# The last layer's 32 gate, query and key projections in a Strassen stage of their own, handed on through DRAM

## The chip, the cores and the metric

One Trainium2 chip, one core of it. The metric is device time in microseconds for one execution, compared between the kernel before and the kernel after. No collective is involved; what follows is one instruction stream on each of TensorE (PE), VectorE (DVE), ScalarE (ACT) and GpSimd (POOL), and one queue of DMAs issued by SyncE (SP).

## The reference

Two blocks run on 1024 tokens of width 1024 (fp32). The first block has an attention layer, an MLP, an LRU layer and a second MLP; the second block has one layer, the last of the kernel and the one the change is about:

```
x = rms_norm(x, final_norm)                      # end of the first block
h = x @ w_in      # q 512, k 512, v 1024, gate_a 1024, alpha 16, pool_in 1024, gate_b 1024, merge 2048
log_alpha = log_sigmoid(alpha_low @ w_alpha_up + b_alpha) / 16
o   = _gla_chunked(q / sqrt(128), k, v, log_alpha)       # 4 heads, dk 128, dv 256, chunks of 64
y_a = headwise_norm(o) * gla_norm_g * silu(gate_a)
y_b = _multiscale_pool(pool_in, w_pool_grp, pool_scale) * silu(gate_b)
g_a, g_b = split(sigmoid(merge + b_merge))
y   = (g_a * (y_a @ w_proj_a) + g_b * (y_b @ w_proj_b)) @ w_out
out = layernorm(2**0.25 * x + y)
```

An MLP of the first block is `square(relu(h @ w_up)) @ w_down`. The final norm's factor per token is applied after the projections, since `(x * rs) @ w = rs * (x @ w)`.

## The kernel before

Activations lie transposed: eight tiles `x[k]` of 128 features by 1024 tokens. Every fp32 operand is split into two fp32r parts, `wh, wl` for weights and `xgh, xgl` (called `X`) for the normed activations; a product is three matmuls (`mm3`, lines 154 to 156: high by high, high by low, low by high). An **m-tile** is 128 output features of a projection for all 1024 tokens: `gemm` (line 160) makes 2 halves of 512 columns x 8 k x 3 = 48 matmuls of 128x512 for it. Its weights come by one DMA of 512 KB (`wdma`), one ACT copy (line 122) and one DVE subtraction (line 124).

The stages follow each other in program order, each with its own split of the eight PSUM banks. What matters here:

- `mlp_up` (line 645): the up projection by Strassen's algorithm in Winograd's form. 32 m-tiles, in pairs. The first two pairs are made directly (`up(m)`, 4 x 48 matmuls) while DVE and ACT build the sums of quarters of `X` (`sums`: T1, T2, T3, T4). T4 is written over the upper halves (tokens 512 to 1023) of X[0] to X[3] (line 726). Then 14 `unit`s, each a pair of m-tiles, do 7 products of 4 k x 3 matmuls of 128x512 where a direct pair would do 8. `load(u)` forms four half sums of the weights on DVE, and `finish` squares and spills what the down projection needs, with four adds on POOL.
- `gla_mix` (line 1046): the last layer up to `y_b @ w_proj_b`. Its first lines split and square x (`norm`). Then generators are woven: **fills**, which give PE dense work, and **chains**, which are long dependent sequences of small work.
  - Fills (`fill_steps`, line 1216), 40 steps: merge gates 0 to 7; then for each head h two tiles of gate_a, two of pool_in, two of gate_b (with the 256x256 map of the pool group), two more merge gates. Merge gates and gate_a go to DRAM and come back later.
  - `decays` (line 1081): alpha projection, log-sigmoid, a scan per head, spill of G; then `z_tokens` transposes x (all eight tiles still held) into the residual.
  - `qkv(h)` (line 1129): two m-tiles (q, k) and v in eight blocks of 24 matmuls of 128x256. It comes before chain h.
  - `chain(h, q, k, v)` (line 1244), 18 steps: six levels, each POOL differences of G (lines 1268, 1269), ACT exp, DVE q and k products (1271, 1272), PE scores (1253) into one tile `sc` by DVE copies (1260); then eight steps of the running state (PE 1322 to 1327, DVE 1332), a norm, and the scaling by gate_a (1356).
  - The order: 3 fills and the first step of the decays, decays with 5 fills, then for h = 0, 1, 2 `qkv(h)` and chain h with 9 fills, then `qkv(3)`, the first 9 steps of chain 3 with the last 5 fills, then the rest of chain 3, then `merge_b`.
- `merge_b` (line 1378) reads y_b back from DRAM, splits it (lines 256, 257) and makes 8 m-tiles; `merge_out` follows.

The Tile framework turns this into queues: it orders each engine's instructions by program order and by a simulated time, so a later instruction can stand ahead of an earlier one that is not ready there. On the chip each engine then keeps its order. Buffers of 128x1024: 31 of tag A (`a`), 8 of tag B (`b`), and 2 `ws`, 5 `wh`, 5 `wl` for weights. An instruction that needs a buffer waits for the last reader of its former content. X takes 16 of the 31.

Of the kernel before, what the change touches and what calls it, by code (L numbers as in the profile page):

```python
# [8 lines left out]
F32 = mybir.dt.float32  # L9
# [36 lines left out]
class Core:  # L46
# [151 lines left out]
    def stats(self, accs, name, w=T, tok=False, alloc=None):  # L198
# [16 lines left out]
        rt = None  # L215
        if tok:
            nb = w // P
            pt = self.pb("st")
            for b in range(nb):
                nc.tensor.matmul(pt[:, b : b + 1], rs[:, b * P : (b + 1) * P], self.first, start=True, stop=True)  # L220
            rt = self.small(nb, name + "t", bufs=1)
            nc.vector.tensor_copy(rt, pt[:, :nb])
        return rs, rt
# [421 lines left out]
    def mlp_up(self, ly, x, xd, sets):  # L645
        nc, I = self.nc, self.I
        act, tt, stt = nc.scalar.activation, nc.vector.tensor_tensor, nc.vector.scalar_tensor_tensor
        lo, hi = slice(0, HB), slice(HB, T)
        gain = lambda k: self.vec("mlp", 8 * ly + k)
        ng = self.small(8, "ng", bufs=1)  # L650
        nc.vector.tensor_scalar(ng, self.vec("mlp", 8 * ly, 8), -1.0, None, op0=ALU.mult)
        X, acc = [], None
        for k in range(KT):
            sq = self.a("sq")
            act(sq, x[k], AF.Square)
            if acc is None:
                acc = sq
            else:
                tt(acc, acc, sq, op=ALU.add)
            X.append(self.split(x[k], "xg", scale=gain(k)))  # L660
            xd.append(self.spill("x", x[k]))
        factors = []

        def rs():

            if not factors:
                factors.append(self.stats([acc], "rs", alloc=self.b)[0])
            return factors[0]
# [16 lines left out]

        def up(m):
            t = self.b("ht")
            self.gemm(self.wload(I["w_up"][ly, m]), X, lambda o, ps: stt(
                t[:, o], ps, 0.0, rs()[:, o], op0=ALU.max, op1=ALU.mult))
            return t  # L690
# [43 lines left out]
        def load(u):  # L734

            a, b = self.wdma(I["w_up"][ly, 2 * u]), self.wdma(I["w_up"][ly, 2 * u + 1])
# [16 lines left out]
        def unit(u):  # L753
# [20 lines left out]
            stt(hn[:, lo], q, 0.0, rs()[:, lo], op0=ALU.min, op1=ALU.mult)  # L774
            stt(hn[:, hi], hn[:, hi], 0.0, rs()[:, hi], op0=ALU.min, op1=ALU.mult)
            product(r, A["s4"], B22, False)
            tt(hm[:, hi], r, cu[:, hi], op=ALU.add)
            stt(hm, hm, 0.0, rs(), op0=ALU.max, op1=ALU.mult)
# [11 lines left out]
        for _ in prev:  # L790
            pass

# [253 lines left out]
    def gla_mix(self, x, early):  # L1046
        F0, FH = 8, (9, 9, 9)
# [3 lines left out]
        X, acc = self.norm(x, lambda k: self.vec("fin", k))  # L1051
        rs = rt = None

        def factors():

            nonlocal rs, rt
            if rs is None:
                rs, rt = self.stats([acc], "rs", tok=True)

        zd = []  # L1060
        hbm = self.cp.tile([P, 16], F32, tag="hbm", name="hbm")
        ts(hbm, self.vec("bm", 0, 16), 0.5, None, op0=ALU.mult)
# [13 lines left out]
        def proj(name, i, f):  # L1076
            def evac(o, ps):
                factors()
                f(ps)

            self.gemm(load(name, i), X, evac)
# [3 lines left out]
        def decays():  # L1085
# [24 lines left out]
            yield  # L1110
            for h in range(4):
                az, mn, rm, g = self.a("az"), self.a("mn"), self.a("rm"), self.a("G")
# [10 lines left out]
                nc.gpsimd.memset(rm, 1.0)  # L1123
                nc.gpsimd.memset(rm.rearrange("p (c t) -> p c t", t=P)[:, :, 0:1], 0.0)
# [3 lines left out]
            yield from self.z_tokens(x, rt, zd)  # L1128

        def qkv(h):  # L1130
            q, k = self.a("gq"), self.a("gk")
            proj("gq", h, lambda ps: stt(q, ps, 128 ** -0.5, rs, op0=ALU.mult, op1=ALU.mult))
            proj("gk", h, lambda ps: tt(k, ps, rs, op=ALU.mult))
            v = [self.a("gv") for _ in range(2)]
            wb = [self.wload(I["w_gv"][h, kb]) for kb in range(2)]
# [8 lines left out]
            return q, k, v  # L1144
# [12 lines left out]
        yad, ybd, thd = [None] * 8, [None] * 8, [None] * 16  # L1157

        def merge_gate(m):
            def f(ps):  # L1160
                t = self.b("mg")
                tt(t, ps, rs, op=ALU.mult)
                act(t, t, AF.Tanh, scale=0.5, bias=hbm[:, m : m + 1])
                thd[m] = self.spill("th", t)
            proj("mg", m, f)
# [46 lines left out]
        def gate_a(m):  # L1212
            gate("ga", m)
            sga["ga", m] = self.spill("ga", sga["ga", m])
# [14 lines left out]
        def fills():  # L1229
# [7 lines left out]
            for i, _ in enumerate(fill_steps()):  # L1237
                if i + 1 in ends:
                    ahead(("gq", ends.index(i + 1)))
                elif i + 1 < len(keys):  # L1240
                    ahead(*keys[i + 1])
# [401 lines left out]
```

## Time and profile before

| what | value |
|---|---|
| median of 3 runs | 3298.57 us (3297.83 to 3303.44) |
| the profiled execution's own time | 3297.68 us |
| its span, first to last instruction | 3295.6 us |
| PE busy | 3237.1 us, 98% of the span |
| DVE, ACT, POOL busy | 65%, 42%, 16% of the span |

A busy PE counts modelled ends of overlapping matmuls (a 128x512 matmul is shown with 0.39 us but the next starts 0.23 us after it), so work on PE is best counted from start to start. Rows of stretches give for each engine the time busy and, in brackets, the number of instructions.

### The profile page before, as it was taken

To read this page: it belongs to the slowest core of one execution; us is meant where nothing else is said; L and a number is where in the kernel's file an instruction comes from. 1 tells how busy PE (TensorE), PEld (TensorE's weight loads), DVE (VectorE), ACT (ScalarE), POOL (GpSimd) and SP (SyncE) were. 2 spreads that over 40 slices of the span, in tenths; PEclk is the share of its full clock that TensorE was granted. 3 is DMA by queue.
4 is the path that set the end of the run, shared out by engine and by line. 5 is a ranking of instruction groups with operands and counts; after the bars stand their busy time and mean duration, and the time that the engine had idled before them with its cause. 6 is when DMAs were issued, how large, how long until landed. Compare 5 with 4: busy or idle time off the path is not lost.

```text
span 3295.6 us, 40225 instructions
## 1 busy us (share of the span) xinstructions
PE 3237.1 (98%) x15484; PEld 2701.1 (82%) x15484; DVE 2150.4 (65%) x2740; ACT 1397.0 (42%) x1957; POOL 529.8 (16%) x576
## 2 busy tenths in 40 slices
PE   8998999999999999999999999999999999999998
PEld 6887787888888888778788888888888888887887
DVE  7588877766686669996686567675554544548334
ACT  5335775434443358864533344434322222224121
POOL 0135551322200000001022220000020111112020
PEclk9998999999999999999999999999999999999999
DMA  5455322344786742253334478663413121225532
GB/s 207 130 182 187 76 53 83 126 149 154 268 293 224 236 155 95 102 188 132 122 109 157 154 243 294 231 206 96 166 52 103 58 90 64 77 83 210 180 122 90
DMA packets 155887, 489.93 MB, mean 149 GB/s; under 512 B 17584, under 2 KB 23216, under 8 KB 155696
## 3 DMA queue, kind: packets, MB, share of 16 engines
q1 hardware_dynamic: 155696, 487.38, 43.8%
q8 instruction: 121, 1.98, 0.2%
q14 instruction: 70, 0.57, 0.1%
HBM read 346.80 MB, written 140.51 MB: 148 GB/s over the span
## 4 chain that ended last, share of the span: by engine, by line
PE 84%; DVE 6%; issue 1%; ACT 1%; DMA 1%; POOL 0%; SPq 0%; DVEq 0%; ACTq 0%
PE mm L154 24%; PE mm L155 24%; PE mm L156 24%; PE sc L1253 1%; PE pt L611 1%; PE mo L154 1%; PE mo L156 1%; PE mo L155 1%; DVE lr L986 1%; DVE wl L124 1%; PE po L617 1%; PE po L618 1%; PE sc L584 1%; PE sc L585 0%; PE po L1322 0%
## 5 line engine op out<-in xcount | busy, mean ns | idle before, releaser
L154 PE MATMUL mm<-xgh,wh 128*128 128x512 f32 x1888 | 743.2, 394 | 0.9 <-ACT misc L770 0.9
L156 PE MATMUL mm<-xgh,wl 128*128 128x512 f32 x1888 | 739.8, 392 | 0.0
L155 PE MATMUL mm<-xgl,wh 128*128 128x512 f32 x1888 | 738.9, 391 | 0.0
L122 ACT ACTIVATE wh<-ws 128x1024 fp32r<-128x1024 f32 x231 | 244.0, 1057 | 537.9 <-PE mm L155 379.8
L154 PEld LDWEIGHTS mm<-xgh,wh 128*128 128x128 f32 x1888 | 355.0, 188 | 75.5 <-ACT misc L770 1.8
L156 PEld LDWEIGHTS mm<-xgh,wl 128*128 128x128 f32 x1888 | 354.8, 188 | 73.3 <-issue 0.5
L155 PEld LDWEIGHTS mm<-xgl,wh 128*128 128x128 f32 x1888 | 355.0, 188 | 72.5 <-issue 1.2
L124 DVE TENSOR_TENSOR wl<-ws,wh 128x1024 fp32r<-128x1024 f32 x231 | 290.7, 1259 | 96.2 <-ACT wh L122 95.7
L155 PE MATMUL mm<-T,wh 128*128 128x512 f32 x512 | 199.3, 389 | 0.0
L351 POOL TENSOR_SCALAR mP<-mP,mr 128x256 f32<-128x256 f32 x64 | 36.6, 585 | 833.3 <-DVE mr L348 830.4
L154 PE MATMUL mm<-oh,wh 128*128 128x512 f32 x384 | 151.1, 399 | 2.7 <-DVE mqr L179 2.2
L156 PE MATMUL mm<-oh,wl 128*128 128x512 f32 x384 | 150.7, 392 | 0.0
L155 PE MATMUL mm<-B,wh 128*128 128x512 f32 x384 | 149.5, 389 | 0.0
L746 DVE TENSOR_TENSOR wl<-ws,wh 128x512 fp32r<-128x512 f32 x84 | 70.5, 866 | 85.1 <-ACT wh L745 71.6
L745 ACT ACTIVATE wh<-ws 128x512 fp32r<-128x512 f32 x84 | 50.0, 627 | 176.6 <-PE mm L155 94.8
L155 PEld LDWEIGHTS mm<-T,wh 128*128 128x128 f32 x512 | 96.1, 188 | 19.9
L677 POOL TENSOR_TENSOR ta<-hm 128x512 f32<-128x512 f32 x28 | 40.0, 1430 | 398.9 <-ACT hm L674 344.9
L155 PE MATMUL mm<-y,wh 128*128 128x512 f32 x256 | 100.2, 391 | 0.0
L156 PE MATMUL mm<-yh,wl 128*128 128x512 f32 x256 | 100.2, 391 | 0.0
L154 PE MATMUL mm<-yh,wh 128*128 128x512 f32 x256 | 99.3, 393 | 0.0
L395 DVE TENSOR_TENSOR xr<-mm,xr 128x512 f32<-128x512 f32 (+1 forms) x80 | 63.3, 793 | 51.3 <-PE mm L156 50.9
L852 DVE TENSOR_TENSOR x<-x,mm 128x512 f32<-128x512 f32 x112 | 76.4, 682 | 31.2 <-PE mm L156 31.2
(532 smaller groups left out, 7526.9 us busy)
## 6 DMA issues: line engine op xcount, KB each, us to landing
ws<-in_w_down SPq DMA_DIRECT2D x144, 512.0 KB, 4.0
ws<-in_w_up SPq DMA_DIRECT2D x64, 512.0 KB, 3.8
T<-h SPq DMA_DIRECT2D x64, 512.0 KB, 5.5
B<-h SPq DMA_DIRECT2D x48, 512.0 KB, 5.5
h<-ta SPq DMA_DIRECT2D x64, 256.0 KB, 2.0
h<-tb SPq DMA_DIRECT2D x64, 256.0 KB, 3.3
h<-hn SPq DMA_DIRECT2D x56, 256.0 KB, 2.7
ws<-in_w_out SPq DMA_DIRECT2D x24, 512.0 KB, 3.6
```

What stands on the lines that cost most here:

```text
L122: nc.scalar.activation(wh, st, AF.Copy)
L124: (lo or nc.vector).tensor_tensor(wl, st, f32(wh), op=ALU.subtract)
L154: mm(ps, wh, xh, start=start, stop=False)
L155: mm(ps, wh, xl, start=False, stop=False)
L156: mm(ps, wl, xh, start=False, stop=stop)
L351: nc.gpsimd.tensor_scalar(Ps[:, s], Ps[:, s], ri[:, j : j + 1], 1.0, op0=ALU.mult, op1=ALU.mult)
L395: self.gemm((wh[:, c], wl[:, c]), X, lambda o, ps: nc.vector.tensor_tensor(x[m][:, o], ps, x[m][:, o], op=ALU.add))
L584: nc.tensor.matmul(ps[:, :w], Q2[h][:, qsl], K2[0][:, ksl], start=True, stop=False)
L677: add(ta[:, lo], hm[:, lo], hm[:, hi], op=ALU.subtract)
L745: act(h[:, n], t[:, n], AF.Copy)
L746: tt(l[:, n], t[:, n], f32(h)[:, n], op=ALU.subtract)
L852: tt(t, t, ps, op=ALU.subtract if i else ALU.add)
```

## The change

The body of `mlp_up` becomes `up_stage`, used by both MLPs as before and by a new stage `gates` ahead of `gla_mix`. `gates` makes 32 m-tiles: 16 merge gates, 8 of gate_a, 4 of q, 4 of k. The first four directly, the other 28 in 14 units. `finish` applies tanh or the scaling and spills all 32 to DRAM. x is spilled (8 tiles) at the start, as in `mlp_up`. Before T4 overwrites the upper halves of X[0] to X[3], these are copied to DRAM (8 DMAs of 256 KB, `kept`), and read back after the last unit (8 more), since v, pool_in, gate_b and alpha still need them. Weights of v for head 0 are loaded ahead of that.

In `gla_mix` there are 24 fills instead of 40: for each head v in two steps, two tiles of pool_in, two of gate_b. q, k and gate_a are read from DRAM in the chain, x from DRAM in `decays` (8 tiles). A chain computes the factors of level n+1 (`prep`) ahead of the scores of level n, and has 19 steps. Six fills go with the decays, 5, 5 and 4 with chains 0 to 2, 4 with the first ten steps of chain 3, and the rest of chain 3 is woven with six tiles of `merge_b`. The reset mask `rm` is made once and not per head.

```diff
-    def mlp_up(self, ly, x, xd, sets):
+    def up_stage(self, x, xd, vec, wsrc, ops, finish, kept=None):
...
         for j, t4 in zip((0, 2), t4s):
             for i, s in enumerate((lo, hi)):
                 h, l = (p[:, hi] for p in X[j + i])
+                if kept is not None:
+                    d = self.tc.dram_tile([P, T], F32, name=self.uid("B12"))
+                    for p, sd in ((h, lo), (l, hi)):
+                        nc.sync.dma_start(d[:, sd], f32(p))
+                    kept.append(d)
                 act(h, t4[:, s], AF.Copy)
                 tt(l, t4[:, s], f32(h), op=ALU.subtract)
...
+    def gates(self, x, early, G):
...
+        tiles = [(n, m) for n, c in (("mg", 16), ("ga", 8), ("gq", 4), ("gk", 4)) for m in range(c)]
...
+        def finish(u, hm, hn):
+            for i, t in ((2 * u, hm), (2 * u + 1, hn)):
+                n, m = tiles[i]
+                if n == "mg":
+                    act(t, t, AF.Tanh, scale=0.5, bias=hbm[:, m : m + 1])
+                elif n == "ga":
+                    v = self.b("gth")
+                    act(v, t, AF.Tanh, scale=0.5)
+                    stt(t, v, 1.0, t, op0=ALU.add, op1=ALU.mult)
+                elif n == "gq":
+                    act(t, t, AF.Copy, scale=128 ** -0.5)
+                G[n, m] = self.spill(n, t)
+
+        xd, kept = [], []
+        with self.banks(mm=(HB, 8), st="mm"):
+            X, rs = self.up_stage(x, xd, lambda k, n=1: self.vec("fin", k, n), wsrc,
+                                  ((1.0, ALU.mult), (-1.0, ALU.mult)), finish, kept)
+        for kb in range(2):
+            early["gv", (0, kb)] = self.wload(I["w_gv"][0, kb])
+        for k, d in enumerate(kept):
+            for p, s in zip(X[k], (slice(0, HB), slice(HB, T))):
+                nc.sync.dma_start(f32(p)[:, HB:], d[:, s])
+        return X, rs, xd
...
-        F0, FH = 8, (9, 9, 9)
+        F0, FH = 6, (5, 5, 4)
...
+            xs = [self.reload("x", d) for d in xd]
...
         def fill_steps():
-            for m in range(8):
-                merge_gate(m)
-                yield
             for h in range(4):
-                for i in range(2):
-                    gate_a(2 * h + i)
-                    yield
+                yield from values(h)
                 yield from pool_group(h)
-                for i in range(2):
-                    merge_gate(8 + 2 * h + i)
-                    yield
...
-        def chain(h, q, k, v):
-            g = self.reload("G", G[h])
+        def chain(h):
+            g, q, k = (self.reload(n, d) for n, d in (("G", G[h]), ("gq", gd["gq", h]), ("gk", gd["gk", h])))
...
+            nxt = prep(levels[0])
+            yield
+            for li in range(6):
+                cur = nxt
+                if li < 5:
+                    nxt = prep(levels[li + 1])
...
         for h in range(3):
-            q, k, v = qkv(h)
-            weave(take(f, FH[h]), FH[h], chain(h, q, k, v), 18)
-        q, k, v = qkv(3)
-        g = chain(3, q, k, v)
-        weave(f, 32 - sum(FH), take(g, 9), 9)
+            weave(take(f, FH[h]), FH[h], chain(h), 19)
+        g = chain(3)
+        weave(f, 24 - F0 - sum(FH), take(g, 10), 10)
         mgd = []
         mb = self.merge_b(ybd, thd, mgd)
         next(mb)
-        for _ in g:
-            pass
+        weave(take(mb, 6), 6, g, 9)
```

## Rows read from the trace of the kernel before

**Rows 1.** The profile's page: engine busy times over the span, and the shares by engine of the chain that ended last.
```profile
PE 3237.1 (98%) x15484; PEld 2701.1 (82%) x15484; DVE 2150.4 (65%) x2740; ACT 1397.0 (42%) x1957; POOL 529.8 (16%) x576
...
PE 84%; DVE 6%; issue 1%; ACT 1%; DMA 1%; POOL 0%; SPq 0%; DVEq 0%; ACTq 0%
```

**Rows 2.** Stretches of the trace. Columns: start and end, length, then busy time and number of instructions of PE, of its weight loads, of DVE, ACT and POOL, the granted clock, the DMA share and GB/s. In order: `mlp_up` of the second MLP in the middle; LRU layer; attention layer; `gla_mix` up to chain 0; chains 0, 1, 2; chain 3 to the last fills; the hand-over to `merge_b`; `merge_b`.
```profile
1660.00:1900.00 240.00, 239.54 (x1057) 198.12 (x1056) 159.44 (x199) 92.86 (x126) 67.43 (x47) 1.00 0.43 143
1240.00:1440.00 200.00, 192.08 (x832) 156.33 (x831) 197.59 (x162) 163.71 (x153) 0.00 (x0) 0.99 0.28 97
...
400.00:520.00 120.00, 113.74 (x584) 94.17 (x583) 85.16 (x228) 85.17 (x211) 64.84 (x128) 0.97 0.19 49
2253.00:2385.00 132.00, 132.00 (x632) 109.99 (x632) 70.50 (x71) 53.20 (x53) 4.28 (x8) 1.00 0.39 132
2385.00:2545.00 160.00, 160.00 (x859) 137.49 (x859) 76.53 (x92) 43.03 (x62) 22.08 (x23) 1.00 0.24 78
2545.00:2705.00 160.00, 160.00 (x874) 138.74 (x873) 82.15 (x92) 40.36 (x56) 21.84 (x15) 1.00 0.24 77
2705.00:2860.00 155.00, 155.00 (x853) 133.86 (x852) 84.45 (x95) 41.73 (x54) 30.25 (x23) 1.00 0.22 71
2860.00:2995.00 135.00, 135.00 (x727) 116.72 (x726) 74.63 (x82) 32.87 (x46) 30.31 (x23) 1.00 0.24 78
2995.00:3020.00 25.00, 19.63 (x115) 14.20 (x113) 18.05 (x28) 12.85 (x21) 0.00 (x0) 1.00 0.97 379
3020.00:3112.00 92.00, 91.99 (x413) 75.67 (x412) 39.84 (x43) 24.34 (x32) 4.62 (x8) 1.00 0.56 197
```

**Rows 3.** Single matmuls in order of time: start, duration, engine, line, operands. First and last of 24 matmuls of 128x512 in a unit of `mlp_up`.
```profile
1932.00 0.39 PE L154 MATMUL mm<-xgh,wh 128*128 128x512 f32 x1
...
1937.21 0.39 PE L156 MATMUL mm<-xgh,wl 128*128 128x512 f32 x1
```

**Rows 4.** The same view for `qkv(0)`: first and last of 24 matmuls of 128x256 of v.
```profile
2388.16 0.28 PE L154 MATMUL mm<-wh,xgh 128*128 128x256 f32 x1
...
2390.92 0.28 PE L156 MATMUL mm<-wh,xgl 128*128 128x256 f32 x1
```

**Rows 5.** What PE waited for in 1637 to 1962 us (all of the second MLP's `mlp_up`): who waited for whom, us in total, times, longest.
```profile
PE mm L154 <- ACT misc L770: 0.5, 1, 0.5
```

**Rows 6.** The same view for 2253 to 3112 us (`gla_mix`).
```profile
PE sc L1253 <- DVE sc L1260: 3.8, 4, 1.6
PE pu L1327 <- DVE misc L1332: 1.1, 2, 0.6
```

**Rows 7.** DVE evacuations of the 32 m-tiles (16 merge gates; gate_a and gate_b together; q; k): count, duration in ns (least, median, most), first and last start.
```profile
L1162 DVE TENSOR_TENSOR mg<-mm,rs x16: 1200/1224/1225, 2271.9 to 3002.4; 128x1024 f32<-128x1024 f32 x16
L1151 DVE TENSOR_TENSOR gg<-mm,rs x16: 1204/1224/1225, 2417.1 to 2968.9; 128x1024 f32<-128x1024 f32 x16
L1132 DVE SCALAR_TENSOR_TENSOR gq<-mm,rs x4: 1211/1218/1225, 2372.9 to 2895.5; 128x1024 f32<-128x1024 f32 x4
L1133 DVE TENSOR_TENSOR gk<-mm,rs x4: 1224/1224/1227, 2382.0 to 2906.9; 128x1024 f32<-128x1024 f32 x4
```

**Rows 8.** Groups of DVE instructions in 2385 to 2995 us: count, busy us and mean ns, idle before.
```profile
L124 DVE TENSOR_TENSOR wl<-ws,wh 128x1024 fp32r<-128x1024 f32 x49 | 63.8, 1303 | 47.5 <-ACT wh L122 47.4
...
L1153 DVE SCALAR_TENSOR_TENSOR gg<-gth,gg 128x1024 f32<-128x1024 f32 x16 | 20.2, 1261 | 0.0
```

**Rows 9.** The chains' instructions: count, duration in ns, first and last start; under line 1268, what POOL's idle time before it ended with (us, times).
```profile
L1271 DVE TENSOR_TENSOR gqe<-gq,ge x24: 1198/1220/2911, 2401.2 to 2992.5; 128x1024 f32<-128x1024 f32 x24
...
L1268 POOL TENSOR_TENSOR ge<-G x24: 1037/1043/2111, 2390.2 to 2980.1; 128x512 f32<-128x512 f32 x24
...
  PE sc L1253: 57.6, 6
...
L1327 PE MATMUL pu<-gv,kgT x56: 378/379/484, 2487.9 to 3019.4; 128*128 128x256 f32 x56
...
L1356 DVE SCALAR_TENSOR_TENSOR ga<-sc,hgn,ga x16: 737/750/753, 2540.8 to 3060.7; 128x512 f32<-128x512 f32 x16
```

**Rows 10.** Single instructions in order of time: POOL, the first of chain 3; DVE, the last copy of chain 0's state output and its last scaling by gate_a.
```profile
2950.33 1.52 POOL L1268 TENSOR_TENSOR ge<-G 128x512 f32<-128x512 f32 x1 [52.07 <-DMA G<-G]
...
2530.74 0.42 DVE L1335 COPY go<-po 128x256 f32<-128x256 f32 x1 [4.94 <-PE po L1324]
...
2547.61 1.41 DVE L1356 SCALAR_TENSOR_TENSOR ga<-sc,hgn,ga 128x512 f32<-128x512 f32 x2
```

**Rows 11.** All engines in order of time around the end of the fills: last projection matmul, first read of y_b, first matmul of `merge_b`.
```profile
3000.27 0.40 PE L156 MATMUL mm<-xgh,wl 128*128 128x512 f32 x1
...
3006.49 0.44 SPq L248 DMA_DIRECT2D y<-yb  x1
...
3019.45 0.81 PE L154 MATMUL mm<-yh,wh 128*128 128x512 f32 x2
```

**Rows 12.** DMA issues: count, KB each, median us from issue to landing (first row: `mlp_up`; others: `gla_mix`).
```profile
h<-ta SPq DMA_DIRECT2D x30, 256.0 KB, 2.0
...
G<-G SPq DMA_DIRECT2D x8, 512.0 KB, 4.4
...
y<-yb SPq DMA_DIRECT2D x8, 512.0 KB, 8.5
```

More of the change, by code (lines that the diff above doesn't have):

```diff
@@ L214, in stats, with tok @@
         self.rsqrt_newton(rs, v, rs, t)
[L215 to L223, printed above, removed]
+        return rs, self.tok(rs, name + "t", w) if tok else None
+    def tok(self, rs, name, w=T):
+        nc, nb = self.nc, w // P
+        pt = self.pb("st")
+        for b in range(nb):
+            nc.tensor.matmul(pt[:, b : b + 1], rs[:, b * P : (b + 1) * P], self.first, start=True, stop=True)
+        rt = self.small(nb, name, bufs=1)
+        nc.vector.tensor_copy(rt, pt[:, :nb])
+        return rt
     def norm(self, x, gain, before=()):
@@ L645, in mlp_up @@
     def mlp_up(self, ly, x, xd, sets):
-        nc, I = self.nc, self.I
-        act, tt, stt = nc.scalar.activation, nc.vector.tensor_tensor, nc.vector.scalar_tensor_tensor
+        nc, act = self.nc, self.nc.scalar.activation
         lo, hi = slice(0, HB), slice(HB, T)
[L649 to L668, printed above, removed]
         def finish(u, hm, hn):
@@ L791, in mlp_up @@
             pass
+        return X, rs()
     def mlp_down(self, ly, xd, sets, ahead):
@@ L1044, in z_tokens, with wsrc, gla_mix @@
             yield
-    def gla_mix(self, x, early):
-        F0, FH = 8, (9, 9, 9)
+    def gates(self, x, early, G):
+        nc, I = self.nc, self.I
+        act, stt = nc.scalar.activation, nc.vector.scalar_tensor_tensor
+        hbm = self.cp.tile([P, 16], F32, tag="hbm", name="hbm")
+        nc.vector.tensor_scalar(hbm, self.vec("bm", 0, 16), 0.5, None, op0=ALU.mult)
+        tiles = [(n, m) for n, c in (("mg", 16), ("ga", 8), ("gq", 4), ("gk", 4)) for m in range(c)]
+        def wsrc(i):
+            n, m = tiles[i]
+            return early.pop((n, m), None) or self.wdma(I["w_" + n][m])
+        def finish(u, hm, hn):
+            for i, t in ((2 * u, hm), (2 * u + 1, hn)):
+                n, m = tiles[i]
+                if n == "mg":
[17 more added lines that the diff above has]
+        return X, rs, xd
+    def gla_mix(self, X, rs, xd, gd, early):
+        F0, FH = 6, (5, 5, 4)
         nc, I = self.nc, self.I
@@ L1127, in decays, with values @@
                 yield
[L1128 to L1135, printed above, removed]
+            yield from self.z_tokens(xs, rt, zd)
+        V = {}
+        def values(h):
+            v = V[h] = [self.a("gv") for _ in range(2)]
+            wb = [load("gv", (h, kb)) for kb in range(2)]
             for b in range(8):
@@ L1155, in gate @@
             proj(name, m, f)
[L1157 to L1165, printed above, removed]
+        yad, ybd, thd = [None] * 8, [None] * 8, [gd["mg", m] for m in range(16)]
         def pool_group(g):
@@ L1525, in tile_kernel @@
             x = K.mlp(1, x, ahead_gla)
+            gd = {}
+            X, rs, xd = K.gates(x, early, gd)
             with K.banks(mm=(T, 2), sc=(HB, 2), po=(HB, 1), pu=(HB, 1), st="sc"):
-                r = K.gla_mix(x, early)
+                r = K.gla_mix(X, rs, xd, gd, early)
             with K.banks(mm=(T, 2), mo=(HB, 4)):
```

87 lines of the change are left out of this document (50 added, 37 removed).

## The prediction, before any run of the changed kernel

> **What bounds the kernel now.** Start with the page's busy times and its chain [rows 1]: PE is busy 98% of the span and carries 84% of the chain that ended last. The kernel is bound by the number of matmuls nearly everywhere; an edit is worth what it takes off PE's queue, less the gaps it opens there. Then read the stretches [rows 2]. From 2253 to 3112 us, the 859 us of `gla_mix`, PE's busy time falls short in one place only, the hand-over to `merge_b` (19.63 of 25.00 us). DVE is next, 75 to 86 us in stretches of 135 to 160. The lists of waits say the same from the other side: PE waited 0.5 us in the second MLP's `mlp_up` [rows 5], the model of the new stage, and 3.8 and 1.1 us in `gla_mix` [rows 6]. So the questions are how many matmuls go, and whether a `gla_mix` with 16 fewer fills, and q and k gone too, still feeds PE while the chains run.
>
> **Matmuls.** Before, 32 m-tiles x 48 = 1536 of 128x512. After, 4 x 48 + 14 units x 7 products x 12 = 1368; 168 fewer. From start to start one takes (1937.21 - 1932.00) / 23 = 0.2265 us [rows 3]; in the middle of `mlp_up`, with all that a unit does, 240 us / 1057 = 0.2271 [rows 2]. 168 x 0.2265 = **-38.1 us**. The stage then takes 1368 x 0.2265 = 310 us, and `gla_mix` keeps 859 - 1536 x 0.2265 = 511 us.
>
> **The added work of the stage, at nothing.** The sums of X, the half sums of weights and the splits are those of `mlp_up`, where DVE is busy 159.4 of 240 us and PE waits 0.5 us [rows 2, 5]. New against it: a tanh in place of a square on ACT, one more DVE operation of 1.26 us for each of 8 gate_a tiles [rows 8]; gone: 67 us of POOL adds [rows 2]. The evacuations (1.22 us each [rows 7]) move along with the tiles. Spills: 32 tiles instead of 24, and x; a unit issues two 512 KB spills where one of `mlp_up` issues seven of 256 KB. The copies of X's upper halves must have left before T4 is written; 256 KB lands in 2.0 us [rows 12], and T4 is first used five products, 60 matmuls or 13.6 us, into the units. Without that cover it would cost those 2 us once. Taken: 0, bounds 0 to +2.
>
> **The end of the stage.** Eight reads of 256 KB (2.1 MB) into X may start when the last product with T4 is done. They stand on SP's queue behind two weight loads of v and ahead of eight reads of x. PE still has 12 matmuls of that unit (2.7 us), four v blocks that need only tokens 0 to 511, 96 matmuls at (2390.92 - 2388.16) / 23 = 0.12 us [rows 4], 11.5 us, and 16 of alpha (3.6 us): 17.8 us of cover. The reads need 2.0 us plus 2.1 MB at 379 GB/s (5.5 us) or, slow, 143 GB/s (14.7 us) [rows 2, 12]: 7.5 to 16.7 us. Hidden, closely; if queue order takes the v blocks away as cover, up to 10 us. Taken: **+2**, bounds 0 to +10. What would be late next is the alpha projection, and with it G and chain 0.
>
> **The loads on DVE and POOL in the chains.** Out of 2385 to 3020 us go 24 m-tiles: PE 24 x 10.9 = 261 us; DVE 24 splits of 1.30, 32 operations of 1.22 to 1.26 [rows 7, 8], about 70 us. The fills of head 0 (192 v matmuls, 4 m-tiles, 24 pool-map matmuls: 72 us of PE, an estimated 30 of DVE) move ahead of chain 0; six `merge_b` tiles (65 us, with splits 25 of DVE) move in. The four chains then meet 635 - 261 - 72 + 65 = 367 us of PE, DVE's 335.8 - 70 - 30 + 25 = 261 us (71%) and POOL's 104.5 us (28%) [rows 2]. PE remains the longest. The LRU layer shows what DVE may carry before PE suffers: at 197.6 of 200 us PE was still busy 192.1 [rows 2], a loss of 4%.
>
> **The latency of the chains** is the term I am least sure of. Up to now each chain had about 160 us of PE work around it; now it has 367 / 4 = 92. A chain is one sequence over POOL, ACT, DVE and PE, and the next needs most of its buffers. How short can it be? Chain 3, the densest, began at 2950.3 [rows 10], had its last state update at 3019.4 and its last scaling at 3060.7 [rows 9]: 111 us with the end of the latter. But between those two, `merge_b`'s splits stood ahead of it on DVE and ACT; chain 0 needed 2530.7 to 2549.0, 18 us, from its last state output to its last scaling [rows 10]. So L, the time of one chain, lies between 69 + 18 = 87 and 111 us. What precedes chain 0 takes PE 132 - 10 x 10.9 + 72 = 95 us [rows 2] and two `merge_b` tiles follow (22 us); if chains do not overlap, `gla_mix` lasts 95 + 4L + 22, or PE's 511 if that is more. It binds above L = 98.5 and costs 4 us per us from there. Towards the upper end speaks that DVE will be fuller, and that buffers are short: POOL already waited 57.6 us in six places for scores that held a level's buffers [rows 9]. After the change X (16), two heads' v (4), g, q, k, sc (4) and a pool group (4) leave 3 of 31, one level's worth, so the factors cannot run far ahead. Towards the lower end: computing them ahead takes the wait from scores to factors out of the sequence, and q and k come early from DRAM. I take L = 100, a little above the middle: **+6**; bounds 0 (L = 87) and +50 (L = 111).
>
> **The hand-over to `merge_b`, unchanged.** PE's last projection matmul started at 3000.27, the first read of y_b was issued at 3006.49, the first y matmul came at 3019.45 [rows 11]: the y buffers are X's, so the reads (8.5 us to land [rows 12]) cannot start while projections still read X. The last fill is now a gate_b tile instead of a merge gate, and the order fills, y, `merge_b` is the same. The 5.4 us of PE idle there [rows 2] may stay or be filled by more chain work: taken 0, bounds -5.4 to +10 (the spill of y_b, so far covered by two merge gates, lands in view).
>
> **Sum.** Against the profiled execution's own 3297.68 us: -38.1 + 0 + 2 + 6 + 0 = -30.1, so 3267.6 us. That execution lies 0.9 us below the median of the runs; on their scale 3268 us, -0.9%. Differences under 0.2% (6.6 us) would be no change by what a measurement of this kernel can tell.
>
> **Rivals.** (1) *The chains hide wholly.* L stays below 98.5, the reads are covered, the merge tiles fill the hand-over: 3297.7 - 38.1 - 5.4 to 0 = 3254 to 3260. For it: DVE at 71% leaves room to place a chain's steps early; against it: the three free buffers.
> (2) *DVE and POOL hold each other up.* In the chains DVE would have 261 us and POOL 104.5: together 365 of 367. If neither could run during the other, DVE would in effect be at 99%, and the LRU row's 4% of 367 us, 15 us, is lost on top of the 2 and 6: 3283. The signs are mixed: L1271 takes 1.22 us at the median and up to 2.91 [rows 9], but in 400 to 520 us DVE and POOL are busy 85.2 + 64.8 = 150 us within 120 [rows 2], so they do run at once for 30 us of it at least. The Trainium skill's page "SBUF — State Buffer", section "Who interferes with whom", states this as a rule: a VectorE instruction with two SBUF inputs and a GpSimd instruction that reads SBUF share a port pair as an exclusive lock. By that rule the q and k products and the splits would queue behind POOL's differences; the 2.91 us agree with it, the 150 in 120 us do not contradict it, since that stage's DVE work partly reads PSUM.
> (3) *The chains in series set the end*, the case on the other side. Place: chain h + 1 waits for chain h's buffers, and chain 0 for the decays and x's eight buffers to be free. Price: 4 us per us of L above 98.5; it eats the gain at L = 98.5 + 36 / 4 = 107.5 and makes the kernel slower beyond. At chain 3's 111 us: 95 + 444 + 22 = 561 instead of 511, +50, so 3312. For it: 111 us was measured, with DVE less full; against it: 41 of those 111 us lie after the last state update, where chain 0 needed about 18.
> (4) *The stage saves nothing*, because additions stop PE: `mlp_up` is against it [rows 5]; it would leave about 3298.
>
> **How the numbers follow.** Forecast (3262 to 3278): 0.45. Rival 1: 0.25. Rival 2 (3278 to 3292): 0.10. Rival 3: 0.10 slower by over 0.2%, and 0.08 for L between 106 and 109, within it. Rival 4: 0.02, within it. Faster 0.45 + 0.25 + 0.10 = 0.80; same 0.10; slower 0.10. The range runs from all terms at their best, 3254 less 2 for the median's spread, to L = 106.5 (95 + 426 + 22 = 543, +32): 3297.7 - 38.1 + 2 + 32 = 3294. It leaves out about 0.18, nearly all above.
>
> **What the profile after would show.** Matmuls: 15484 - 168 = 15316. The new stage about 310 us long, at 0.227 us a matmul, PE waits of a us or two. If the reads are late: a PE gap before alpha's second half, ended by a DMA. If the chains are short enough: from a chain's first POOL operation to its last scaling by gate_a under 98 us, PE idle in `gla_mix` below 15 us. If rival 3 holds: PE waiting for DVE copies of scores or of the state, tens of us in all, POOL waiting for PE's scores, and DVE's share in the chains well under 71%. Rival 2: the q and k products at a median well over 1.22 us. The granted clock, 1.00 in all of `gla_mix` [rows 2], would fall where PE waits long, as in the attention layer, 0.97 with 6.3 of 120 us idle [rows 2]. The prediction is wrong if buffers or SP's queue make a chain much longer than any before, or if the order of the queues puts fills behind a chain that waits.

## The result, and the profile after

The changed kernel takes 3342.1 us (median of four runs, 3341.0 to 3344.4) against 3298.2 us for the kernel before on the same chip: ratio 1.0134, 95% interval 1.0122 to 1.0146. It is 1.3% slower; the prediction was 0.9% faster, and its range ended at 3294.

The page of the profile after, busy times and the shares of the chain that ended last:

```profile
PE 3228.7 (97%) x15316; PEld 2690.4 (80%) x15316; DVE 2264.7 (68%) x2927; ACT 1457.3 (44%) x2061; POOL 524.9 (16%) x570
...
PE 78%; DVE 7%; issue 3%; ACT 2%; DMA 2%; POOL 1%; SPq 0%; ACTq 0%; DVEq 0%; POOLq 0%
```

The 168 matmuls are gone (15316 against 15484 in [rows 1]), but PE's busy time fell by 8.4 us only, and its share of the chain from 84% to 78%. So in the last part PE waits more than before, and what it does there it does more slowly. Where, the stretches say (columns as in [rows 2]): the new stage, from its first matmul to its last; from its end to the first POOL operation of chain 0; chains 0, 1 and 2, each to the first POOL operation of the next; chain 3 to the first matmul of `merge_b`; `merge_b`.

```profile
2256.90:2575.10 318.20, 314.32 (x1373) 258.35 (x1372) 205.48 (x269) 126.73 (x165) 1.07 (x2) 0.99 0.33 108
2575.10:2697.70 122.60, 106.97 (x606) 91.32 (x605) 63.81 (x70) 42.25 (x49) 0.00 (x0) 0.93 0.46 165
2697.70:2787.30 89.60, 87.87 (x526) 77.59 (x525) 62.64 (x72) 27.41 (x41) 22.12 (x15) 1.00 0.24 78
2787.30:2894.60 107.30, 96.21 (x553) 84.23 (x553) 64.73 (x88) 30.75 (x54) 21.22 (x24) 0.94 0.24 80
2894.60:3002.70 108.10, 95.13 (x565) 84.33 (x564) 65.53 (x88) 32.96 (x55) 34.99 (x32) 0.94 0.20 70
3002.70:3063.60 60.90, 47.41 (x253) 40.61 (x252) 53.87 (x56) 19.27 (x26) 25.09 (x15) 0.86 0.48 174
3063.60:3158.60 95.00, 95.00 (x428) 78.45 (x427) 42.18 (x48) 27.43 (x38) 3.65 (x8) 1.00 0.55 189
```

From 2575.1 to 3158.6 us the rest of `gla_mix` takes 583.5 us; the prediction had 511 as PE's time and as the least. The 72.5 us more are two things. PE stands idle: length less busy time over these rows is 54.9 us, against 5.4 in [rows 2], so 49.5. And it is busy for 528.6 us with matmuls that, by [rows 2], took 853.6 - 1536 x 0.2265 = 505.7 before: 22.9, mostly in stretches with a granted clock of 0.86 to 0.94 where it was 1.00. The stage takes 318.2 us where its 32 tiles took 1536 x 0.2265 = 347.9, so it gives back 29.7. 72.5 less 29.7 is 42.8; the two profiled spans lie 47.0 apart (3342.6 and 3295.6), of which 3.9 come ahead of the stage's first matmul (2256.9 against 2253.0), and the medians 43.9.

What PE waited for in 2565 to 3165 us (columns as in [rows 6]); lines 1278, 1285 and 1297 are the scores, their DVE copies and the k products, 1388 the transposes of the heads' outputs behind the norm on POOL (1379):

```profile
PE sc L1278 <- DVE sc L1285: 15.6, 7, 4.0
PE sc L1278 <- DVE gke L1297: 10.5, 4, 4.3
PE sc L1388 <- POOL go L1379: 8.1, 4, 4.3
PE sc L1062 <- DVE zt L1064: 5.2, 5, 4.5
PE sc L1062 <- DVE mn L1168: 4.7, 1, 4.7
```

[Rows 6] had 4.9 us in all. Cut the same part by another measure and the idle time shows as a comb:

```profile
2780.00:2830.00 50.00, 38.91 (x244) 34.75 (x243) 34.24 (x41) 16.93 (x27) 21.14 (x23) 0.86 0.24 85
2830.00:2900.00 70.00, 70.00 (x379) 60.59 (x379) 39.58 (x59) 20.63 (x38) 4.84 (x5) 1.00 0.29 98
2900.00:2955.00 55.00, 42.46 (x280) 38.91 (x279) 38.18 (x44) 16.70 (x24) 24.56 (x20) 0.88 0.13 48
2955.00:3010.00 55.00, 54.57 (x300) 47.13 (x298) 32.10 (x46) 15.44 (x29) 12.98 (x13) 1.00 0.26 87
3010.00:3060.00 50.00, 36.68 (x203) 32.27 (x203) 44.63 (x46) 14.55 (x17) 17.79 (x11) 0.83 0.45 161
```

PE is full for 55 to 70 us, then a quarter idle for 50 to 55. The full parts are mostly the eight state steps of a chain, where about 20 projection matmuls stand between two steps. The bare ones are the end of that chain and levels of the next that have no projection between them: the first three in chain 1, all six in chain 2, the last three in chain 3. PE in order of time at the first such place:

```profile
2801.67 4.22 PE L1388 MATMUL sc<-ident,go 128*128 128x128 f32 x12 [4.27 <-POOL go L1379]
2806.31 1.11 PE L1388 MATMUL sc<-ident,go 128*128 128x128 f32 x4 [0.42 <-DVE ga L1390]
2807.22 5.32 PE L1278 MATMUL sc<-gqe,gke 128*128 128x128 f32 x32
2816.87 3.61 PE L1278 MATMUL sc<-gqe,gke 128*128 128x128 f32 x16 [4.33 <-DVE gke L1297]
2820.13 0.51 PE L154 MATMUL mm<-wh,xgh 128*128 128x256 f32 x1
```

Chain 0's last transposes wait for POOL's norm, and since they stand ahead on PE's queue, chain 1's scores wait with them; the third level then waits for operands of its own. With 2820.13 the projections are back.

### The profile page after: what moved, and what is told of

It is laid out like the page before. It is cut to its first block, busy times and chain, and to the rows that moved or that the text cites. A ratio compares the mean times of both kernels' runs of the same rounds, so it can differ in the third digit from the quotient of the medians.

```text
span 3342.6 us, 40337 instructions
## 1 busy us (share of the span) xinstructions
PE 3228.7 (97%) x15316; PEld 2690.4 (80%) x15316; DVE 2264.7 (68%) x2927; ACT 1457.3 (44%) x2061; POOL 524.9 (16%) x570
## 4 chain that ended last, share of the span: by engine, by line
PE 78%; DVE 7%; issue 3%; ACT 2%; DMA 2%; POOL 1%; SPq 0%; ACTq 0%; DVEq 0%; POOLq 0%
PE mm L154 22%; PE mm L155 22%; PE mm L156 22%; PE sc L1278 1%; PE pt L613 1%; PE mo L156 1%; PE mo L154 1%; PE mo L155 1%; DVE lr L1008 1%; DVE wl L124 1%; PE po L620 1%; PE po L619 1%; DVE gke L1297 1%; PE sc L586 0%; PE sc L587 0%
## 5 line engine op out<-in xcount | busy, mean ns | idle before, releaser
L154 PE MATMUL mm<-xgh,wh 128*128 128x512 f32 x1664 | 654.2, 393 | 2.0 <-ACT misc L791 1.6
L156 PE MATMUL mm<-xgh,wl 128*128 128x512 f32 x1664 | 649.8, 391 | 0.0
L155 PE MATMUL mm<-xgl,wh 128*128 128x512 f32 x1664 | 649.7, 391 | 0.0
L766 ACT ACTIVATE wh<-S 128x1024 fp32r<-128x1024 f32 x84 | 88.6, 1059 | 77.7 <-PE mm L155 59.5
L154 PE MATMUL mm<-T3h,wh 128*128 128x512 f32 x296 | 115.9, 391 | 1.8 <-ACT cu L786 1.8
L156 PE MATMUL mm<-T3h,wl 128*128 128x512 f32 x296 | 115.7, 391 | 0.0
L154 PE MATMUL mm<-T1h,wh 128*128 128x512 f32 x296 | 115.1, 389 | 0.0
L156 PE MATMUL mm<-T1h,wl 128*128 128x512 f32 x296 | 115.1, 389 | 0.0
L154 PE MATMUL mm<-T2h,wh 128*128 128x512 f32 x296 | 115.1, 389 | 0.0
L156 PE MATMUL mm<-T2h,wl 128*128 128x512 f32 x296 | 115.1, 389 | 0.0
```

Of the source, the lines that this page charges most:

```text
L154: mm(ps, wh, xh, start=start, stop=False)
L155: mm(ps, wh, xl, start=False, stop=False)
L156: mm(ps, wl, xh, start=False, stop=stop)
L766: act(h[:, n], t[:, n], AF.Copy)
```

## The experiments

Three theories: **A**, the chains are serial and there are too few projections to lay beside them; **B**, DVE and POOL are full; **C**, buffers held by the work ahead. Times are medians beside those of the kernel before, 3297.7 to 3298.6 us in these comparisons.

**z_late**: the 64 transposes of x and the reload of x move from ahead of chain 0 to the last two tiles of `merge_b`.

```diff
-            xs = [self.reload("x", d) for d in xd]
...
-            yield from self.z_tokens(xs, rt, zd)
...
-        weave(take(mb, 6), 6, g, 9)
-        for _ in mb:
-            pass
+        weave(take(mb, 6), 6, g, 9)
+        xs = [self.reload("x", d) for d in xd]
+        weave(mb, 2, self.z_tokens(xs, rt, zd), 8)
```

> The residual transposes of x (z_tokens) and the eight reads of x they need are moved from the decays to behind chain 3, beside the last two tiles of merge_b. Theory A (the decays and chains are one long series, and PE has too few projections beside it; x's eight buffers hold up chain 0): chain 0 starts some 30 to 45 us earlier than the 2697.7 us of the changed kernel, the stretch from 2666 to 2694 us in which PE did little but transposes goes, and the time falls by 20 to 35 us, to 3307 to 3322. Rival B (the vector engines are simply full in this part, so work that is moved within it changes nothing): 3337 to 3347.

Measured: 3339.3 us, ratio 1.0126 (1.0111 to 1.0141). Chain 0 did start 30 us earlier, at 2667.9, and `merge_b` 28 us earlier, so x's buffers and the transposes did hold up chain 0. But the starts of the chains lie 89.7, 107.5 and 108.1 us apart as before, and at the end the transposes are bare again (17.4 of 26.7 us busy):

```profile
3133.30:3160.00 26.70, 17.39 (x73) 11.50 (x72) 18.64 (x21) 9.51 (x9) 0.00 (x0) 0.81 0.86 334
```

The loss was moved, not removed: a bare stretch costs wherever it lies. The time is the one that B expected and not A's; it is fills8 that tells the two apart.

**fills8**: eight of the sixteen merge gates leave the stage (24 tiles) and are single projections again, two for each head.

```diff
-        tiles = [(n, m) for n, c in (("mg", 16), ("ga", 8), ("gq", 4), ("gk", 4)) for m in range(c)]
+        tiles = [(n, m) for n, c in (("mg", 8), ("ga", 8), ("gq", 4), ("gk", 4)) for m in range(c)]
...
-        F0, FH = 6, (5, 5, 4)
+        F0, FH = 8, (7, 7, 6)
...
                 yield from pool_group(h)
+                for i in range(2):
+                    merge_gate(8 + 2 * h + i)
+                    yield
```

> Eight merge gates (8 to 15, two per head) go back from the Strassen stage to the fills of gla_mix; the stage keeps 24 m-tiles in 12 pairs. The stage gets shorter by 4 units x 84 matmuls x 0.2265 us = 76 us, gla_mix gets 8 x 48 x 0.2265 = 87 us of PE work. Theory A (too few projections beside the decays and chains, about 80 us of gaps): most of the 87 us falls into the gaps, 60 to 80 us of it, so 3342 - 76 + 87 - 70 = 3283, range 3270 to 3295, faster than the kernel before. Rival B (vector engines full): the eight tiles bring about 20 us more of DVE work into the same part and the gaps stay: 3342 - 76 + 87 = 3353 or more.

Measured: **3290.0 us** (ten runs), ratio 0.9978 (0.9969 to 0.9987): 52 us less than the changed kernel, with 48 matmuls more, and faster than the kernel before. From chain 0's start to `merge_b`, this kernel:

```profile
2628.40:3013.80 385.40, 379.01 (x2184) 329.18 (x2182) 263.13 (x315) 124.46 (x186) 100.57 (x84) 0.99 0.31 106
```

and the changed one:

```profile
2697.70:3063.60 365.90, 326.62 (x1892) 286.75 (x1890) 246.77 (x303) 110.39 (x174) 103.42 (x84) 0.94 0.27 92
```

The stretch is 19.5 us longer and holds 52.4 us more of PE: 6.4 us idle instead of 39.3. DVE has more to do, not less, and at the same share (68% and 67%). That is against B: it expected 3353. It is what A expected (3270 to 3295).

**no_prep**: the factors of a level made in its own step, not a level ahead.

```diff
-            nxt = prep(levels[0])
-            yield
             for li in range(6):
-                cur = nxt
-                if li < 5:
-                    nxt = prep(levels[li + 1])
+                cur = prep(levels[li])
```

> One part undone: a chain computes the factors of a level just ahead of its own scores, as in the kernel before (18 steps), all else as in the changed kernel. Theory A with chains as the limit: each of the four chains gets 3 to 8 us longer, so 3354 to 3374. Rival C (too few buffers are free for the factors to run ahead, or they hold buffers that others need): no change, 3336 to 3348, or a little faster.

Measured: 3334.5 us, ratio 1.0107 (1.0090 to 1.0123), 8 us less than the changed kernel, where A expected at least 12 more; the distances are 92.5, 100.1 and 107.9 us. C has a part in it, a small one.

**fills8_z** joins z_late and fills8.

> Both edits together: eight merge gates as fills, and the residual transposes behind chain 3. Theory A: if the gaps by the decays and those by the chains are separate, both gains add in part, 3265 to 3280; if the eight fills already cover the decays, the same as with the fills alone. Rival B: as for the fills alone, about 3353.

Measured: 3298.3 us, ratio 1.0004 (0.9994 to 1.0013), 8 us worse than fills8 alone: beside the chains PE idles no less (7.3 us in 382.4), and the transposes, covered there by 32 steps of projections, are bare at the end.

**state_dense**: the projections beside chains 0 to 2 woven with the first nine of a chain's 19 steps only.

```diff
-            weave(take(f, FH[h]), FH[h], chain(h), 19)
+            g = chain(h)
+            weave(take(f, FH[h]), FH[h], take(g, 9), 9)
+            for _ in g:
+                pass
```

> Projections are woven only with the first nine steps of chains 0 to 2 (the six levels of the scores), and the recurrent state's steps then follow each other with nothing between. Theory A (the chains run in series, and TensorE has its projections at the wrong places: in the state's steps, which then take 44 to 51 us, and none under the six levels of the next chain): the distance of two chains falls from 107 to 75-95 us, and the time falls by 30 to 60 us, to 3282-3312. Theory B (the vector engines are full): nothing to gain from the order, 3337-3347. Theory C (buffers that the work ahead holds): the levels still wait, the state's steps shorten, and what is won there is lost in the levels, 3325-3347.

Measured: 3327.2 us, ratio 1.0084 (1.0069 to 1.0099), 15 us less than the changed kernel: in C's range, and half of the least that A expected. The distances are 86.7, 110.4 and 89.8 us. What PE waits for, in 2565 to 3165 us:

```profile
PE sc L1388 <- POOL go L1379: 12.7, 4, 5.1
PE sc L1278 <- DVE gke L1297: 7.0, 2, 3.9
...
PE sc L1278 <- DVE sc L1285: 5.3, 3, 2.8
```

The levels wait less (12.3 instead of 26.1 us), the ends of the chains more (12.7 instead of 8.1). So it is C's time without C's reason, by which the levels would still wait.

**levels4** leaves out two of the six levels.

```diff
-            levels = (64, 32, 16, 8, 4, 2)
+            levels = (64, 32, 16, 8)
```

> Leaves out the two smallest of the six levels of the scores in each of the four chains (the output is not the reference's). That takes 128 matmuls of 128x128 off TensorE, 58.8 us / 384 = 0.153 us each, 19.6 us in all. If TensorE's own work set the time of this part, the time would fall by 20 us, to 3322. Theory A (the chains' latency sets it): each level left out is worth its whole passage, some 7 us (six levels took 42 to 45 us where they ran bare), 8 levels 56 us, to 3280-3295.

Measured: 3311.0 us, ratio 1.0031 (1.0022 to 1.0041), 31 us less than the changed kernel: 19.6 of PE's work and 11 of waiting, 3.9 us for a level and not 7. Neither expectation holds. A level's latency counts, but on the mean half of it; chain 0's two levels, for one, had cover.

**fills8_np** joins fills8 and no_prep.

> Eight merge gates back as single projections among the chains (a stage of 24 tiles), and the operands of a level made in its own step, not one level ahead. The first alone gave 3290, the second alone took 8 us from the changed kernel. If prep ahead costs by the buffers that it holds, whatever lies beside it: 3280-3284. If it only cost where TensorE had nothing else (theory A), eight more projections cover it already: 3288-3293.

Measured: 3299.2 us, ratio 1.0003 (0.9994 to 1.0013), 9 us worse than fills8, which neither outcome allowed for: PE idles 14.3 us beside the chains instead of 6.4. With PE nearly covered, making factors ahead is worth its buffers. That it cost 8 us in the changed kernel is measured; why there is not settled.

**fills16**: all sixteen merge gates as projections, a stage of 16 tiles.

```diff
-        F0, FH = 6, (5, 5, 4)
+        F0, FH = 10, (10, 9, 9)
...
                 yield from pool_group(h)
+                for i in range(4):
+                    merge_gate((8 + 4 * h + i) % 16)
+                    yield
```

> All sixteen merge gates back as single projections among the chains, a stage of 16 tiles (first gates, queries, keys). Half of the saving of the stage is left, 19 us; the projections that lie among the chains are 40 tiles' steps, not 24. Theory A (too few projections to hide the chains): TensorE's losses beside the chains fall to those of the kernel before, and the whole 19 us show: 3276-3284. Theory B (the vector engines full, which the merge gates' evacuations load again): no better than with eight, 3290-3300.

Measured: 3293.1 us (ten runs), ratio 0.9980 (0.9970 to 0.9989). PE idles 7.9 us in 446.8 beside the chains. So A's step holds, its sum does not: the kernel has 72 matmuls less than before, worth 16.3 us, and shows 5. Of the other 11 the trace shows ten: PE idles 2.5 us more beside the chains than before, and the stage takes 165.2 us, 7.6 more than its 696 matmuls at 0.2265. DVE is busy 60% beside the chains.

```profile
2255.80:2421.00 165.20, 160.77 (x701) 131.04 (x700) 116.20 (x149) 66.53 (x85) 1.07 (x2) 1.00 0.31 106
```

More projections than fills8 has buy nothing.

**warm**: useless matmuls behind the levels, meant for the bare stretches. (As built, five follow each level, not each half of one: 90, or 20.4 us at the full rate.)

```diff
                         nc.vector.copy_predicated(s3, m3, p3)
+                if h:
+                    pw = self.pb("mm")
+                    for i in range(5):
+                        nc.tensor.matmul(pw[:, :HB], X[0][0][:, :P], X[1][0][:, :HB], start=True, stop=True)
```

> The changed kernel with 180 matmuls of 128x512 more whose results nobody reads: five behind each half of each level of the scores in chains 1 to 3, where TensorE is else bare. At the full rate they take 180 x 0.2265 = 40.8 us of TensorE. If the loss is the chains' latency alone, the useless matmuls lie in waits that are there anyway and the time stays at 3335-3350. If a good part of the loss is TensorE's own slower clock in the bare stretches (windows of the changed kernel: granted clock 0.79 to 0.88, 96.2 us busy where the same matmuls take 83 at the full rate), work that keeps it from waiting gives that part back, and the time falls, to 3315-3333. If neither (TensorE's time is on the path there): 3355-3385.

Measured: 3347.8 us (3342.4 to 3352.3), ratio 1.0148 (1.0133 to 1.0163), beside 1.0134 of the changed kernel (the intervals overlap): 0 to 10 us more for 20.4 us of PE work. Chains 1 and 2:

```profile
2780.00:2887.30 107.30, 98.57 (x579) 86.81 (x579) 65.39 (x88) 30.61 (x54) 23.66 (x23) 0.94 0.21 72
2887.30:2996.10 108.80, 99.37 (x601) 86.87 (x600) 64.37 (x84) 33.13 (x54) 33.48 (x32) 0.98 0.23 75
```

The same lengths as without them (107.3 and 108.1), with 26 and 36 matmuls more in each. But the queue does not hold all of them where the program has them. In chain 1 none lies in the bare stretch, whose clock stays low, so there the clock is not tested; in chain 2 ten lie behind the transposes and some ahead of them, and the clock up to the state steps rose from 0.88 to 0.97. In order: warm's bare stretch of chain 1; chain 2 up to its state steps in warm, and in the changed kernel.

```profile
2796.40:2812.90 16.50, 12.94 (x65) 10.71 (x66) 11.53 (x13) 3.90 (x5) 11.26 (x13) 0.71 0.15 64
2887.30:2938.00 50.70, 43.50 (x275) 37.95 (x274) 40.22 (x42) 15.98 (x18) 27.80 (x23) 0.97 0.28 93
...
2894.60:2945.00 50.40, 37.93 (x242) 34.59 (x241) 38.91 (x43) 16.37 (x20) 29.32 (x23) 0.88 0.21 77
```

So in chain 2 a faster clock shortened nothing. For chain 1 the changed kernel's chain that ended last runs through the slow matmuls themselves:

```profile
2801.67 3.81 PE sc L1388 x10
...
2807.43 5.13 PE sc L1278 x32
...
2816.87 3.61 PE sc L1278 x16
...
2826.27 1.79 PE sc L1278 x16
```

Sixteen scores take 3.61 us there and 1.79 ten us later. At that pace the three pieces would take 6.5 us instead of 12.6 (an estimate from these rows). What the slower clock costs by itself is open.

**fills8_sd** and **fills12_sd** join state_dense with eight, and with twelve, merge gates as projections.

> Both moves together: eight merge gates back as single projections, and all projections woven with the first nine steps of chains 0 to 2. If the places of the projections still matter with 32 steps of them (TensorE lost 9.7 us each between the starts of chains 1, 2 and 3 there): 3281-3287. If eight more cover the chains wherever they lie: 3288-3293. If the state's steps, now with nothing between, become the wait: above 3293.

> As the kernel before it in this list, with twelve merge gates back (a stage of 20 tiles, 36 steps of projections). It gives up 4 x 1.2 = 4.8 us of the stage's saving against eight. If the places are what is left, 3284-3291, a little above that kernel; if the number still is, 3279-3286, below it.

Measured: 3330.8 us, ratio 1.0095 (1.0080 to 1.0110), and 3325.4 us, ratio 1.0083 (1.0067 to 1.0100). The third outcome: 41 us worse than fills8 with the same work. Twelve instead of eight make no difference that can be told, where 4.8 us either way had been expected. Nor is fills12_sd quite as described: its weave for chain 3 has 4 - F0 - sum(FH) where 36 was meant, so in program order three of chain 3's four projections come behind its first ten steps. In both traces the last projection matmuls start before chain 3's scores, at 2984 us in fills8_sd and 2992 in fills12_sd. What PE waits for in fills8_sd (lines 1391, 1400, 1290 and 1309 here are 1379, 1388, 1278 and 1297 of the changed kernel):

```profile
PE sc L1400 <- POOL go L1391: 15.7, 3, 5.6
PE sc L1290 <- DVE gke L1309: 6.9, 1, 6.9
```

**fills8_tail** gives each of chains 0 to 2 two of its projections back at its end, between the norm on POOL and the transposes.

```diff
+            weave(take(f, FH[h] - 2), FH[h] - 2, take(g, 9), 9)
+            for _ in take(g, 9):
+                pass
+            for _ in take(f, 2):
+                pass
+            next(g)
```

> Eight merge gates back as single projections, as in the kernel that gave 3290, with the projections of chains 0 to 2 at other places: five (four in chain 2) over the first nine steps, none in the state's eight steps, and two between the norm of the heads' outputs on GpSimd and the transposes that wait for it. With all of them in the first nine steps that wait alone took 15.7 us of TensorE in three times and the whole kernel was 40 us slower than with them spread evenly. If that wait at the end of a chain is what the dense order lost, the time comes back to 3280-3295. If the bare stretch between two chains is long whatever lies in it (first level's operands, 6.9 us, and the hand-over to chain 3): 3305-3325.

Measured: 3307.7 us, ratio 1.0029 (1.0017 to 1.0041): 23 of the 41 us come back, its second outcome. The wait for POOL is still 10.2 us in four times, so two projections there don't cover it, and the state's steps are bare.

All of them, from chain 0's start to `merge_b` (one row of stretches for each kernel):

| kernel | steps of projections | time, us | length | PE idle | clock |
|---|---|---|---|---|---|
| before | 40 and q, k, v | 3298 | 629.3 | 5.4 | 1.00 |
| fills16 | 40 | 3293 | 446.8 | 7.9 | 0.99 |
| fills8 | 32 | 3290 | 385.4 | 6.4 | 0.99 |
| fills8_z | 32 | 3298 | 382.4 | 7.3 | 1.00 |
| fills8_np | 32 | 3299 | 396.6 | 14.3 | 0.97 |
| fills8_tail | 32, uneven | 3308 | 403.9 | 18.8 | 0.97 |
| fills8_sd | 32, early | 3331 | 422.1 | 32.9 | 0.95 |
| fills12_sd | 36, early | 3325 | 452.4 | 32.1 | 0.95 |
| state_dense | 24, early | 3327 | 353.3 | 27.5 | 0.95 |
| no_prep | 24 | 3334 | 361.5 | 32.0 | 0.93 |
| after | 24 | 3342 | 365.9 | 39.3 | 0.94 |

Two things are needed: enough projections, and one beside each part of a chain. With 32 or 40 spread evenly PE idles 6 to 8 us (14 without factors made ahead, fills8_np). Pushed into the first half of a chain they leave the second half bare, and then it idles 27 to 33 us whether there are 24, 32 or 36. With 24 spread evenly it idles 39, or 32 without factors made ahead. Not varied is what lets a chain begin: for chains 0, 1 and 3 that was the read of G from DRAM.

## Why the prediction was wrong

Three terms failed: the stage (8.2 us over what was taken), what precedes chain 0 (27.6) and the latency of the chains (38.9). Less the 2 us taken for the end of the stage that is 72.7; the profiled execution, 3344.4 us, lies 76.7 above the forecast of 3267.6, and 3.9 of the rest lie ahead of the stage.

**What bounds the kernel; the matmuls.** Right: 15316 matmuls. The stage gives back 29.7 of the 38.1 us, so rival 4 is out. (Two readings are off, with no weight in the sum: DVE's "75 to 86 us" are 75 to 84 in [rows 2], and seven spills of 256 KB in each of 14 units make 49 tiles of 512 KB, not 24.)

**The added work of the stage: 0 taken, bounds 0 to +2; 8.2 measured.** 318.2 us against 310. PE waits three times, 3.9 us in all, where [rows 5] had 0.5:

```profile
PE mm L154 <- ACT cu L786: 1.8, 1, 1.8
PE mm L210 <- DVE sq L689: 1.4, 1, 1.4
PE mm L154 <- ACT misc L791: 0.7, 1, 0.7
```

Behind the first, nine matmuls start 0.43 us apart, and four matmuls of the norm (L210), 1.4 us, now stand in the stage. In fills8 the stage takes 242.3 us against 1032 x 0.2265 = 233.7, in fills16 165.2 against 157.6: some 8 us, whatever its size.

**The end of the stage.** Taken +2. No DMA stands among PE's waits in 2565 to 3165 us, though the reads into X were issued late, at 2570.3 to 2574.0. Hidden.

**The loads.** PE was to remain the longest with DVE at 71%; DVE was at 67% (246.8 of 365.9 us). Rival 2 gets nothing: the q products have a median of 1.254 us against 1.220 in [rows 9], and fills8, with more work on DVE, lost less.

**What precedes chain 0: 95 us taken, 122.6 measured.** The 95 were PE's work alone, counted as if PE were full there. But `decays` needs x and its transposes done before x's buffers are free for chain 0, and six projections are used up by 2660; then:

```profile
2660.00:2700.00 40.00, 26.34 (x165) 21.33 (x164) 29.18 (x31) 19.55 (x24) 2.25 (x3) 0.79 0.60 221
```

The third rival named this wait and gave it no price. Of the 27.6 us PE idles 15.6, 7.6 of them for the sums of the decays (`mn`) and 5.2 for the copies of the transposes (`zt`); 77 v matmuls of head 1, 9.2 us at 0.12, stand ahead of chain 0 and are missing behind it; the rest passed more slowly, at a clock of 0.93. In z_late, without reload and transposes, the same part takes 96.5 us.

**The latency of the chains: L = 100 taken.** The largest, and the one the prediction called its least sure. By its own formula, chain 0's start to the end of `merge_b` is 4L + 22 = 460.9, so L = 109.7, against 111 measured for chain 3 before [rows 9, 10]. The argument for less was that chain 0's tail needed 18 us where chain 3's needed 41; after, the starts of chains 1, 2 and 3 lie 107 to 108 apart. With L = 109.7 the formula gives +45, with the 27.6 the 72.5 us that the part grew. The range ended at L = 106.5, with 95 ahead of it. The third rival, given 0.10, was right in place and sign; its 3312 was 30 us short, since it took L = 111 but still 95 for what precedes chain 0, and nothing for the stage.

That 109.7 comes so close to 111 is in part chance: the first is a mean distance of starts, the second one chain's length. From first POOL operation to last scaling by gate_a, the measure that the prediction named, the chains are 110.5, 131.8, 102.7 and 141.9 us long, none under its 98, and chains 0 and 1 reach 21 and 25 us into the next. Chain 0 and chain 1, first POOL operation and last scaling:

```profile
2697.75 1.04 POOL L1293 TENSOR_TENSOR ge<-G 128x512 f32<-128x512 f32 x1 [129.53 <-DMA G<-G]
...
2807.47 0.75 DVE L1390 SCALAR_TENSOR_TENSOR ga<-sc,hgn,ga 128x512 f32<-128x512 f32 x1 [0.55 <-PE sc L1388]
...
2787.32 1.04 POOL L1293 TENSOR_TENSOR ge<-G 128x512 f32<-128x512 f32 x1 [53.88 <-DMA G<-G]
...
2918.40 0.75 DVE L1390 SCALAR_TENSOR_TENSOR ga<-sc,hgn,ga 128x512 f32<-128x512 f32 x1 [2.56 <-PE sc L1388]
```

What was wrong in the model is more than L. A chain has no length of its own, and the distance to the next is not fixed: 89.6 us (chain 0, whose levels had projections beside them) or 107, and 118 in fills8 where PE is full. The question was not whether 92 us of PE work per chain exceeds L but whether it can be laid beside each step; the weave of 5 projections over 19 steps leaves levels bare.

**The hand-over: 0 taken.** From chain 3's start to `merge_b` PE idles 13.5 us against 5.4 in [rows 2], +8, inside its bounds of -5.4 to +10; but 13.2 of it are waits of chain 3's scores, none is for y, and the 460.9 above holds it.

**The signs named for rival 3.** Waits for copies of scores came (17.2 us in eight times), and so did the slower clock. DVE's share, 67%, is under 71% but not well under. POOL's waits for PE's scores did not grow: 9.1 us in four times against 57.6 in six [rows 9]. The clock was foreseen and not priced; the slower passage of PE's matmuls is at most 22.9 of the 72.5 us. By warm, raising it gained nothing in chain 2; elsewhere that is not tested.

## What to carry to other kernels

Work that is dense on the bounding engine has a second value where it covers a serial chain on the others. Before taking it away, price the cover: lay the chain's measured length against the work that is left for each of its parts, not for the whole, and where a longest length has been measured, take that. Here three quarters of the tiles in the fast stage with eight left as cover beat both kernels (3290 us), while all of them cost 44 us. And price the new stage's own ends: 8 us here, for 16 tiles as for 32. The Trainium skill, "Perfetto Trace Analysis", section "Optimization Strategy", says that where the most contended engine changes over time, interleaving such stretches may help. The runs show a near case: beside the chains PE is still the busiest engine (326.6 of 365.9 us), but it waits on DVE and POOL, and with eight gate projections interleaved the kernel is 52 us faster than with none.

## What the runs showed of the hardware

After a bare stretch PE's matmuls run at half pace for a while. In z_late, where PE had just waited 6 us behind small transposes, matmuls of `merge_out` start 0.43 us apart, 1.9 times the 0.2265 of [rows 3]:

```profile
3148.75 1.22 PE L154 MATMUL mm<-yh,wh 128*128 128x512 f32 x2 [5.97 <-ACT yh L258]
...
3151.03 0.63 PE L155 MATMUL mm<-y,wh 128*128 128x512 f32 x1
3151.46 0.63 PE L156 MATMUL mm<-yh,wl 128*128 128x512 f32 x1
```

The granted clock, in the half-paced stretch and just behind it:

```profile
3148.70:3155.60 6.90, 6.35 (x12) 3.65 (x13) 4.27 (x4) 3.50 (x4) 0.00 (x0) 0.50 1.02 418
3156.30:3162.00 5.70, 5.70 (x27) 4.70 (x26) 4.87 (x4) 3.21 (x4) 0.00 (x0) 1.00 0.29 120
```

0.50 and 1.00 are its two levels, 1.2 and 2.4 GHz. The Trainium skill, "TensorE: Matmul & The Clock Gate", section "Wait — 56ns, not 53.3ns?", gives 426.7 and 215.7 ns from start to start for 512 columns at the two levels; the first agrees with 0.43 us, the second is 5% below what this kernel shows.
